# Reordering the tiles of the longest-lived SBUF pool in a one-layer trunk kernel: u and y ahead of con, rb and par

## The chip, the cores and the metric

The kernel runs on one core of one Trainium2 chip. The metric is the device time of one execution in microseconds; below 0.2% two versions can hardly be told apart here. Engines are named as in the profile: PE is TensorE's matmul, PEld its weight load, DVE is VectorE, ACT is ScalarE, POOL is GpSimd, SP is SyncE, which starts the DMAs.

## The reference, cut to what matters

One layer of a hybrid encoder trunk for 256 tokens of width 2048, all in float32:

```
u = rmsnorm(x, norm_mix_g)
z = u @ w_in                       # 2048 x 5140, four head groups
y = concat(short_gated_conv, multiscale_pool, gated_linear_attention, forgetting_attention)
x = x + y @ w_out                  # 2048 x 2048
u = rmsnorm(x, norm_ffn_g)
x = x + (silu(u @ w_gate) * (u @ w_up)) @ w_down   # 2048 x 5632, 5632 x 2048
```

Nearly all of the arithmetic is in the four large products. The head groups between them are small.

## The kernel before

**Number format.** Every factor of a large product is kept as two float32r parts: a high part, which is the value rounded, and a low part, which is the rest. A product is then three matmuls that add into the same PSUM bank (`three`, lines 135 to 139): weight-high by value-high (L137), weight-high by value-low (L138), weight-low by value-high (L139). Each loads its 128x128 stationary operand anew.

**Weights.** All large weights lie in DRAM as 380 chunks of 512 KB. `stage_through` (L101 to L114) brings a chunk into `raw`, ACT rounds it into `hi` (L113), and DVE subtracts to give `lo` (L114). `raw` has 3 buffers, `hi` and `lo` have 4 each; chunks are staged three ahead of their use. One chunk feeds 24 matmuls of 256 columns, or 12 of 512.

**Values.** `u` holds the normalized input as [128 partitions, 16 blocks of the model width, 2 parts, 256 tokens], `y` the mixer's output in the same shape, 32768 bytes per partition each. Both live in the pool `keep` for the whole kernel, with `xT` (the running x, transposed), `par` (54 columns of gains, biases and other parameters), `con` (960 columns of constants: identity, ones, masks), `rb` and `rcol` (the inverse norms).

**Stages in order.**

- The lead block (`block_lead`, L168) and one more block of 256 columns (`block_fm`): `u` is the moving operand.
- Five blocks of 512 columns (`block_tm`, L183 to L185): here `u` is the stationary operand and the weight parts `hi` and `lo` are the moving ones.
- Eight blocks of `block_fm` with `u` moving, then the output projection, eight blocks with `y` moving.
- Gate and up, 44 blocks with `u` (the first 4) or `y` (the other 40) moving; `y` has been overwritten by the normalized input.
- Down, 8 blocks over the 5632 hidden columns. The high parts of the hidden values overwrite `u` and then `y`; the low parts lie in eleven tiles `hl` of the pool `ffn`, which opens when the mixer's pools have closed. So of each three matmuls two have `u` or `y` as moving operand and the middle one has `hl`.

Small matmuls of the head groups (attention scores, transposes, gates) are placed between the large ones by a list of tasks, a step or two after each chunk. Two of them are named below: L635 multiplies `wsm`, a weight that lies in the room of `y` for a while, as stationary operand by 512 columns of `u`, sixteen times in a row; L526 multiplies a small `sel` by 256 columns of `fhl`, both float32r tiles of the pool `mx`.

**Where a tile lies.** In a pool with one buffer per tile, the tiles lie one behind another in the order in which they are first asked for, each one starting at the next multiple of 32 bytes within a partition. The pools lie one behind another too.

Of the kernel before, what the change touches and what calls it, by code (L numbers as in the profile page):

```python
# [9 lines left out]
F32 = mybir.dt.float32  # L10
# [7 lines left out]
P = 128  # L18
# [19 lines left out]
NPAR = 54  # L38

C_ID, C_ONE, C_CAUS, C_RST, C_CNT, NCON = 0, 128, 384, 640, 896, 960  # L40
# [19 lines left out]
def trunk_kernel(ctx: ExitStack, tc: tile.TileContext, a, out):  # L60
# [3 lines left out]
    keep = ctx.enter_context(tc.tile_pool(name="keep", bufs=1))  # L64
# [10 lines left out]


    xT = keep.tile([P, KT, T], F32, name="xT")
    par = keep.tile([P, NPAR], F32, name="par")
    con = keep.tile([P, NCON], F32, name="con")
    u = keep.tile([P, KT, 2, T], F32R, name="u")  # L80
    y = keep.tile([P, KT, 2, T], F32R, name="y")
    rb = keep.tile([P, T], F32, name="rb")
    rcol = keep.tile([P, 2], F32, name="rcol")

    mixer = ExitStack()
# [769 lines left out]
```

## Time and profile before

| | |
|---|---|
| median of 3 runs | 1118.85 us (1117.97 to 1119.15) |
| the profiled execution | 1118.63 us |
| its span, first to last instruction | 1116.8 us |
| PE busy | 1107.4 us, 99% |
| PEld busy | 1073.3 us, 96% |
| DVE busy | 634.6 us, 57% |
| ACT busy | 487.4 us, 44% |
| DMA | 204.09 MB, mean 183 GB/s |

The span leaves 1.8 us of the execution outside. Matmuls overlap in the records: one is listed with some 281 ns, while the next starts some 118 ns after it. So a matmul's cost on the path is the step from its start to the next one's start, and a busy PE says nothing on whether PE runs at its best.

### The profile page before, as it was taken

Reading aid. Unit: us, or ns where it says so; the run is one execution under the profiler, and the core shown is the slowest. Engines: PE = TensorE matmul, PEld = TensorE weight load, DVE = VectorE, ACT = ScalarE, POOL = GpSimd, SP = SyncE. Lnnn points to the kernel's source line nnn. Section 1 sums busy time; section 2 is a strip of 40 time slices with the busy share of each in tenths; the row PEclk is TensorE's granted clock in tenths of the full one; section 3 lists DMA queues with packets and bytes.
Section 4 is the critical chain, followed back from the end, with each engine's and each line's share of the span. In section 5 each row is a group of like instructions: output and inputs, shape, how many; then the busy total and the mean of one; then the engine's idle time right before and its main releaser. Section 6 shows DMA issues by size and latency. Waiting matters only on the chain.

```text
span 1116.8 us, 20632 instructions
## 1 busy us (share of the span) xinstructions
PE 1107.4 (99%) x8836; PEld 1073.3 (96%) x8836; DVE 634.6 (57%) x744; ACT 487.4 (44%) x577; POOL 7.0 (1%) x12
## 2 busy tenths in 40 slices
PE   9999999999999999999999999999999999999998
PEld 7777779999999999999999999999999999999998
DVE  7797785688565684445545445454445444444442
ACT  6645453444454554444434434343434433333331
POOL 0000000001000000000000000000000000000000
PEclk9999999999999999999999999999999999999999
DMA  8554445444555556555555555555555566666562
GB/s 302 175 177 153 157 148 184 162 160 151 189 189 184 175 182 195 185 184 183 187 189 189 186 183 181 188 189 189 184 182 186 186 198 198 198 196 193 193 197 82
DMA packets 58908, 204.09 MB, mean 183 GB/s; under 512 B 6576, under 2 KB 8768, under 8 KB 58816
## 3 DMA queue, kind: packets, MB, share of 16 engines
q1 hardware_dynamic: 58672, 202.74, 55.5%
q8 instruction: 69, 1.13, 0.4%
q14 instruction: 23, 0.19, 0.0%
q10 hardware_dynamic: 144, 0.03, 0.0%
HBM read 200.65 MB, written 2.10 MB: 182 GB/s over the span
## 4 chain that ended last, share of the span: by engine, by line
PE 95%; DVE 3%; DMA 1%; issue 1%; ACT 0%; ACTq 0%; DVEq 0%
PE acc L139 28%; PE acc L137 28%; PE acc L138 28%; PE acc L183 3%; PE acc L184 3%; PE acc L185 3%; DVE lo L114 1%; PE misc L383 1%; DMA xT<-in_xT 1%; DMA raw<-in_wall 1%; DMA par<-in_par 0%; ACT hi L113 0%; PE misc L544 0%; PE misc L606 0%; DVE fe L310 0%
## 5 line engine op out<-in xcount | busy, mean ns | idle before, releaser
L114 DVE TENSOR_TENSOR lo<-raw,hi 128x1024 fp32r<-128x1024 f32 (+1 forms) x380 | 462.2, 1218 | 430.8 <-ACT hi L113 429.9
L113 ACT CAST hi<-raw 128x1024 fp32r<-128x1024 f32 (+1 forms) x380 | 394.8, 1040 | 579.5 <-PE acc L138 502.7
L139 PE MATMUL acc<-y,lo 128*128 128x256 f32 x1728 | 485.8, 281 | 0.0
L137 PE MATMUL acc<-y,hi 128*128 128x256 f32 x1728 | 485.7, 281 | 0.0
L138 PE MATMUL acc<-y,hi 128*128 128x256 f32 x1536 | 431.7, 281 | 0.0
L139 PEld LDWEIGHTS acc<-y,lo 128*128 128x128 f32 x1728 | 325.5, 188 | 0.0
L137 PEld LDWEIGHTS acc<-y,hi 128*128 128x128 f32 x1728 | 325.5, 188 | 0.0
L138 PEld LDWEIGHTS acc<-y,hi 128*128 128x128 f32 x1536 | 289.4, 188 | 0.1
L137 PE MATMUL acc<-u,hi 128*128 128x256 f32 x928 | 263.0, 283 | 0.0
L139 PE MATMUL acc<-u,lo 128*128 128x256 f32 x928 | 261.6, 282 | 0.8 <-DVE lo L114 0.8
L138 PE MATMUL acc<-hl,hi 128*128 128x256 f32 x704 | 195.4, 278 | 0.0
L139 PEld LDWEIGHTS acc<-u,lo 128*128 128x128 f32 x928 | 174.5, 188 | 1.0 <-DVE lo L114 1.0
L137 PEld LDWEIGHTS acc<-u,hi 128*128 128x128 f32 x928 | 174.5, 188 | 0.6 <-ACT hi L113 0.2
L138 PEld LDWEIGHTS acc<-hl,hi 128*128 128x128 f32 x704 | 132.2, 188 | 0.0
L138 PE MATMUL acc<-u,hi 128*128 128x256 f32 x416 | 116.9, 281 | 0.0
L138 PEld LDWEIGHTS acc<-u,hi 128*128 128x128 f32 x416 | 78.4, 189 | 0.1
L183 PE MATMUL acc<-hi,u 128*128 128x512 f32 x160 | 65.3, 408 | 0.0
L184 PE MATMUL acc<-hi,u 128*128 128x512 f32 x160 | 63.9, 400 | 0.0
L185 PE MATMUL acc<-lo,u 128*128 128x512 f32 x160 | 63.8, 399 | 0.0
L183 PEld LDWEIGHTS acc<-hi,u 128*128 128x128 f32 x160 | 30.3, 190 | 8.1 <-issue 0.3
L185 PEld LDWEIGHTS acc<-lo,u 128*128 128x128 f32 x160 | 30.4, 190 | 7.4
L184 PEld LDWEIGHTS acc<-hi,u 128*128 128x128 f32 x160 | 30.4, 190 | 6.6
(198 smaller groups left out, 407.7 us busy)
## 6 DMA issues: line engine op xcount, KB each, us to landing
raw<-in_wall SPq DMA_DIRECT2D x372, 512.0 KB, 3.6
xT<-in_xT SPq DMA_DIRECT2D x8, 256.0 KB, 5.5
raw<-in_wall SPq DMA_DIRECT2D x8, 256.0 KB, 5.7
out_T<-g SPq DMA_DIRECT2D x7, 256.0 KB, 4.1
con<-in_con SPq DMA_DIRECT2D x1, 480.0 KB, 5.0
msk_raw<-in_msk SPq DMA_DIRECT2D x1, 448.0 KB, 5.8
poolw<-in_poolw SPq DMA_DIRECT2D x1, 256.0 KB, 5.8
out_T<-n SPq DMA_DIRECT2D x2, 128.0 KB, 1.7
```

Of the source, the lines that this page charges most:

```text
L113: S.copy(out=hi[:, c], in_=raw[:, c])
L114: V.tensor_tensor(out=lo[:, c], in0=raw[:, c], in1=hi[:, c].bitcast(F32), op=ALU.subtract)
L137: PE.matmul(o, lhsT=hi, rhs=x[0], start=first, stop=False, skip_group_check=True)
L138: PE.matmul(o, lhsT=hi, rhs=x[1], start=False, stop=False, skip_group_check=True)
L139: PE.matmul(o, lhsT=lo, rhs=x[0], start=False, stop=last, skip_group_check=True)
L183: PE.matmul(b[t], lhsT=u[:, k, 0, ts], rhs=hi[:, kk], start=k == 0, stop=False)
L184: PE.matmul(b[t], lhsT=u[:, k, 1, ts], rhs=hi[:, kk], start=False, stop=False)
L185: PE.matmul(b[t], lhsT=u[:, k, 0, ts], rhs=lo[:, kk], start=False, stop=k == KT - 1)
L383: PE.matmul(banks[h % 2][:, c * P:(c + 1) * P], lhsT=ke[b, h // 2, st * P:(st + 1) * P], rhs=qe[b, h // 2, tt * P:(tt + 1) * P], start=Tru ...
```

## The change

The two parts of the pool that are not a multiple of 64 bytes long, `par` (216 bytes, 224 with rounding) and with it `con`, no longer lie ahead of `u` and `y`:

```diff
     xT = keep.tile([P, KT, T], F32, name="xT")
-    par = keep.tile([P, NPAR], F32, name="par")
-    con = keep.tile([P, NCON], F32, name="con")
+
     u = keep.tile([P, KT, 2, T], F32R, name="u")
     y = keep.tile([P, KT, 2, T], F32R, name="y")
+    con = keep.tile([P, NCON], F32, name="con")
     rb = keep.tile([P, T], F32, name="rb")
+    par = keep.tile([P, NPAR], F32, name="par")
     rcol = keep.tile([P, 2], F32, name="rcol")
```

The starts of the tiles in a partition, in bytes, as the two built programs have them:

| tile | before | modulo 64 | after | modulo 64 |
|---|---|---|---|---|
| xT | 16512 | 0 | 16512 | 0 |
| par | 32896 | 0 | 103296 | 0 |
| con | 33120 | 32 | 98432 | 0 |
| u | 36960 | 32 | 32896 | 0 |
| y | 69728 | 32 | 65664 | 0 |
| rb | 102496 | 32 | 102272 | 0 |
| rcol | 103520 | 32 | 103520 | 32 |
| hi, lo (8 buffers) | 115840 to 144512 | 0 | the same | 0 |
| fhl (2), sel | 166080, 167104, 168128 | 0 | the same | 0 |
| hl (11 tiles) | 174400 to 215360 | 0 | the same | 0 |

The pool keeps its length, so every tile of every other pool stays where it was. The pieces of `u`, `y`, `hl`, `hi` and `lo` that a matmul reads begin at multiples of 512 bytes within their tiles, so a piece has its tile's place modulo 64. Engine by engine, the instructions of the two programs stand in the same order and are the same but for these addresses; line numbers behind the pool's tiles are higher by 1 after the change.

## Rows read from the trace of the kernel before

**Rows 1.** The page: span, busy us (share, instructions) by engine, and PE's granted clock.

```profile
span 1116.8 us, 20632 instructions
...
PE 1107.4 (99%) x8836; PEld 1073.3 (96%) x8836; DVE 634.6 (57%) x744; ACT 487.4 (44%) x577; POOL 7.0 (1%) x12
...
PEclk9999999999999999999999999999999999999999
```

**Rows 2.** The page: chain that ended last, share of the span by engine and by line.

```profile
PE 95%; DVE 3%; DMA 1%; issue 1%; ACT 0%; ACTq 0%; DVEq 0%
PE acc L139 28%; PE acc L137 28%; PE acc L138 28%; PE acc L183 3%; PE acc L184 3%; PE acc L185 3%; DVE lo L114 1%; PE misc L383 1%; DMA xT<-in_xT 1%; DMA raw<-in_wall 1%; DMA par<-in_par 0%; ACT hi L113 0%; PE misc L544 0%; PE misc L606 0%; DVE fe L310 0%
```

**Rows 3.** Groups of PE's instructions: line, shapes, count | busy us, mean ns | idle before.

```profile
L139 PE MATMUL acc<-y,lo 128*128 128x256 f32 x1728 | 485.8, 281 | 0.0
...
L139 PE MATMUL acc<-u,lo 128*128 128x256 f32 x928 | 261.6, 282 | 0.8 <-DVE lo L114 0.8
L138 PE MATMUL acc<-hl,hi 128*128 128x256 f32 x704 | 195.4, 278 | 0.0
...
L183 PE MATMUL acc<-hi,u 128*128 128x512 f32 x160 | 65.3, 408 | 0.0
```

**Rows 4.** Timeline of PE in gate and up, 24 steps apart: start us, us, instruction.

```profile
599.78 0.28 PE L137 MATMUL acc<-y,hi 128*128 128x256 f32 x1
...
602.62 0.28 PE L137 MATMUL acc<-y,hi 128*128 128x256 f32 x1
```

**Rows 5.** Windows, PE alone: stretch, length, busy us (instructions), clock, DMA share, GB/s.

```profile
500.00:800.00 300.00, 300.00 (x2538) 1.00 0.57 186
900.00:1100.00 200.00, 200.00 (x1700) 1.00 0.60 194
```

**Rows 6.** Timeline of PE in down.

```profile
899.95 0.28 PE L137 MATMUL acc<-u,hi 128*128 128x256 f32 x1
900.07 0.28 PE L138 MATMUL acc<-hl,hi 128*128 128x256 f32 x1
900.18 0.28 PE L139 MATMUL acc<-u,lo 128*128 128x256 f32 x1
900.30 0.28 PE L137 MATMUL acc<-u,hi 128*128 128x256 f32 x1
900.42 0.28 PE L138 MATMUL acc<-hl,hi 128*128 128x256 f32 x1
900.54 0.28 PE L139 MATMUL acc<-u,lo 128*128 128x256 f32 x1
900.66 0.28 PE L137 MATMUL acc<-u,hi 128*128 128x256 f32 x1
900.78 0.28 PE L138 MATMUL acc<-hl,hi 128*128 128x256 f32 x1
900.89 0.28 PE L139 MATMUL acc<-u,lo 128*128 128x256 f32 x1
```

**Rows 7.** Tile hl: count, duration ns min/median/max, first and last start us.

```profile
L138 PE MATMUL acc<-hl,hi x704: 277/278/282, 864.7 to 1113.1; 128*128 128x256 f32 x176
```

**Rows 8.** Timeline of PE in the blocks of 512 columns, 24 steps apart.

```profile
160.75 0.40 PE L183 MATMUL acc<-hi,u 128*128 128x512 f32 x1
...
166.35 0.40 PE L183 MATMUL acc<-hi,u 128*128 128x512 f32 x1
```

**Rows 9.** Timeline of PE around L635, sixteen in one row.

```profile
33.96 3.81 PE L635 MATMUL acc<-u,y 128*128 128x512 f32 x16
37.62 0.40 PE L183 MATMUL acc<-hi,u 128*128 128x512 f32 x1
```

**Rows 10.** Timeline of PE at L526 over windows of growing length: one, then all four.

```profile
208.32 0.38 PE L526 MATMUL misc<-fhl,sel 4*128 4x256 f32 x1
208.32 0.73 PE L526 MATMUL misc<-fhl,sel 4*128 4x256 f32 x4
```

**Rows 11.** Waits of PE: line, releaser: us in total, times, longest us.

```profile
PE misc L482 <- DVE ob L473: 1.9, 1, 1.9
PE misc L217 <- DVE sq L284: 1.4, 1, 1.4
PE misc L243 <- DVE idle L239: 1.2, 1, 1.2
PE acc L139 <- DVE lo L114: 0.8, 1, 0.8
```

**Rows 12.** Windows: stretch, length, PE, PEld, DVE, ACT, POOL busy us (instructions), clock, DMA.

```profile
62.00:137.00 75.00, 75.00 (x415) 58.91 (x414) 60.52 (x89) 35.38 (x41) 0.00 (x0) 1.00 0.50 167
520.00:840.00 320.00, 320.00 (x2707) 320.00 (x2706) 153.00 (x146) 131.25 (x146) 0.00 (x0) 1.00 0.57 185
```

## The prediction, as it stood before the changed kernel was run

> **What bounds the kernel now.** I read the page first, then the groups of PE's instructions, then PE's timeline at five places. PE is busy for 99% of the span at a granted clock that never leaves its upper level for a whole slice [rows 1], and the chain that ended last lies on PE for 95%, nearly all of it in the lines of the large products [rows 2]. PE's waits for other engines are four, 5.3 us in all [rows 11]. So the time is the number of matmuls times the step from one start to the next, and the only thing the change can move on the path is that step. The counts: L139 runs 1728 + 928 = 2656 times with 256 columns, and L137 and L138 as often, of which 704 of L138 have `hl` moving [rows 3]; that is 704 groups of three in down and 7968 - 2112 = 5856 matmuls outside it, all with `u` or `y` moving. L183 to L185 are 480 matmuls of 512 columns.
>
> The steps. In gate and up 24 steps take 2.84 us [rows 4], 118.3 ns each; the count over 300 us says the same, 300 us / 2536 = 118.3 (two or three of the 2538 began before the window) [rows 5]. In down the first and the last of 704 `hl` matmuls are 248.4 us apart [rows 7]: 353.3 ns per group of three, 117.8 each. In the 512-column blocks 24 steps take 5.60 us [rows 8]: 233.3 ns.
>
> [...]
>
> **What the trace says about place.** Down has an experiment built in: same weights, same stationary operands, same shape; only the middle matmul's moving operand lies at 0 modulo 64, where the weights lie too, and the other two lie at 32. The step that begins with an `hl` matmul is read as 0.11, 0.12, 0.11 us, the two others as 0.12 each time [rows 6]. Over all 704 from the first to the last [rows 7] the starts in the trace give 114.2 ns from `hl` to the next, 120.0 from L137 to `hl`, 119.3 from L139 to L137. The records agree in length: 278 ns against 281 and 282 [rows 3].
>
> A second place with 512 columns: L635 has both operands at 32 modulo 64 and takes (37.62 - 33.96) / 16 = 228.8 ns [rows 9]; L183 has its stationary operand at 32 and its moving one at 0 and takes 233.3 [rows 8]. So not the place of one operand alone but a like place of both goes with the short step, in both pairs. After the change both operands lie at 0 in every large product.
>
> A third place speaks against it: L526 has both operands at 0, and its second to fourth end 1.05 - 0.70 = 0.35 us apart from the first, 117 ns each [rows 10], as in the mixed case. [...]
>
> **The change part by part.** It removes and adds no instruction, moves none, and adds no wait. The terms are:
>
> - 5856 matmuls outside down: 118.3 becomes 114.2, the step that the matched operands of down have. 5856 x 4.1 ns = 24.0 us. [...]
> - 704 groups in down: 353.3 becomes 3 x 114.2 = 342.6. 704 x 10.7 = 7.5 us. [...]
> - 480 matmuls of 512 columns: 233.3 becomes 228.8, as L635 has it. 480 x 4.5 = 2.2 us. [...]
> - The lead block's 96 and the first 30 us wait for loads: nothing taken.
> - `con`, `par` and `rb` also move. They are read by small ACT and DVE work and by a few dozen small matmuls. DVE and ACT sit idle for 43% and 56% of the span [rows 1], which covers a few ns either way; I take nothing.
>
> Sum 33.7 us; 1118.6 of the profiled execution less 33.7 gives **1085 us** (that execution lies 0.2 us under the median, so nothing is added).
>
> What could hand some of it back: a chunk's 24 matmuls would take 2.74 us instead of 2.84. In gate and up DVE is busy for 153 of 320 us and ACT for 131, the DMA engines for 57% [rows 12], so the weights' supply has room several times over. In the gated attention DVE is busy for 60.5 of 75 us [rows 12], 81%, and PE's waits at L482 and L217 lie around there [rows 11]. That stretch would gain only some 2 to 3 us, so that is all that can be lost.
>
> [...] The built programs show that before and after every piece of `u` and `y` begins on a multiple of 32 bytes and covers 1024 bytes without a gap; [rows 6] has shorter steps for the operand that lies on 64. [...]
>
> **The rivals.**
>
> 1. *No change: 1118.6.* The short step of `hl` would come from something else that sets it apart: it lies in another tile than its neighbours, and higher in memory. For it: L526 with 117 ns in spite of matched operands [rows 10]. Against it: L635 reads `u` and `y`, low in memory, and also has short steps [rows 9]. That the change does not do what it says is ruled out by the addresses of the built program.
> 2. *A smaller gain: 1105.* A start may be recorded later or earlier with the place of the operand. Then only the sum of the three steps is real: 353.3 - 2 x 118.3 = 116.7 for the matched one. 5856 x 1.6 = 9.4, 704 x (353.3 - 350.1) = 2.3, and 0 to 2.2 for the 512 columns: 12 to 14 us. For it: the steps into `hl` are longer than 118.3, as if lent.
> [...]
> 4. *Slower: 1133.* The step depends on the operand that is about to start, and 114.2 is the price of a mismatched one behind a matched one, while 120, the step into `hl`, is the price of a matched moving operand [rows 6]. All at 120: 5856 x 1.7 = 10.0 and 704 x (360 - 353.3) = 4.7, together 14.7 us more. It decides as soon as every step ends at a matched operand, which is everywhere after the change. Against it: the three steps together are shorter than three without `hl`, 353.3 against 354.9.
>
> **How the numbers follow.** The forecast, 1074 to 1095, gets 0.53: two independent pairs of rows show the matched step, with 256 and 512 columns. The smaller gain, 1095 to 1111, gets 0.28. No change gets 0.11, the larger gain 0.04, slower 0.04. The range 1074 to 1111 takes in the first two, 0.81. Faster by over 0.2% is 0.53 + 0.28 + 0.04 = 0.85, within 0.2% (about what a measurement of this kernel can tell from no change) 0.11, slower 0.04.
>
> **What would show it.** In the timeline of gate and up, 24 steps in about 2.74 us instead of 2.84, all alike; the count of PE in 300 us of that stage about 2630 instead of 2538; in down the first and last `hl` matmul 241 us apart instead of 248.4; in the 512-column blocks 24 steps in 5.49 us instead of 5.60; instruction counts as before, DVE's and ACT's busy time too. A step of 116 to 117 in gate and up says the second rival, 118.3 the first, 120 the fourth. The prediction is wrong in its mechanism if `hl` keeps a step that differs from its neighbours', and wrong in its cover if PE's waits for DVE in the first 170 us grow by more than 3 us.

## The result, and the profile after the change

The changed kernel takes 1124.59 us (median of 6 runs, 1122.85 to 1128.24) against 1118.22 us (6 runs, 1117.11 to 1119.15): a ratio of 1.0067, 95% interval 1.0054 to 1.0080. It is slower by 0.7%, a small loss but clear of the spread, where 1085 us was forecast. Lines of the changed kernel are higher by 1: L138 to L140 are the three matmuls of a large product, L184 to L186 those of the 512-column blocks.

The page of the changed kernel, span, busy time by engine and the chain that ended last; they answer to [rows 1, 2]:

```profile
span 1122.3 us, 20632 instructions
...
PE 1112.7 (99%) x8836; PEld 1082.1 (96%) x8836; DVE 634.5 (57%) x744; ACT 487.0 (43%) x577; POOL 6.9 (1%) x12
...
PE 94%; DVE 2%; DMA 2%; ACT 1%; issue 0%; SPq 0%; ACTq 0%; DVEq 0%
```

The same instructions, DVE and ACT as busy as before, the bound still PE. So it is again the step from one matmul to the next. The windows of PE alone (stretch, length, busy us and instructions, clock, DMA share, GB/s), to be read beside [rows 5]:

```profile
500.00:800.00 300.00, 300.00 (x2503) 1.00 0.56 184
900.00:1100.00 200.00, 200.00 (x1701) 1.00 0.61 196
```

In gate and up there are 2503 matmuls in 300 us where there were 2538; in down as many as before. The timeline of PE gives the steps: in gate and up, 24 steps apart, as [rows 4]; then 18 steps apart in the 512-column blocks, as [rows 8]:

```profile
599.46 0.28 PE L139 MATMUL acc<-y,hi 128*128 128x256 f32 x1
...
602.34 0.28 PE L139 MATMUL acc<-y,hi 128*128 128x256 f32 x1
```

```profile
160.67 0.39 PE L184 MATMUL acc<-hi,u 128*128 128x512 f32 x1
...
164.75 0.39 PE L184 MATMUL acc<-hi,u 128*128 128x512 f32 x1
```

And the tile `hl` (count, ns min/median/max, first and last start), as [rows 7]; 703 steps of a group lie between its first and last start:

```profile
L139 PE MATMUL acc<-hl,hi x704: 279/280/286, 870.2 to 1118.6; 128*128 128x256 f32 x176
```

| step, ns | before | forecast | after |
|---|---|---|---|
| 256 columns, gate and up | 118.3 | 114.2 | 2.88 us / 24 = 120.0 |
| group of three in down | 353.3 | 342.6 | 248.4 us / 703 = 353.3 |
| 512 columns, L183 to L185 | 233.3 | 228.8 | 4.08 us / 18 = 226.7 |

From these steps: 5856 x 1.7 = 10.0 us lost, nothing in down, 480 x 6.6 = 3.2 us gained, together 6.8 us longer by this estimate. The two profiled spans differ by 5.5 us, the medians by 6.4.

### The profile page after: what moved, and what is told of

Same layout as the page of the kernel before. It is cut to its first block, busy times and chain, and to the rows that moved or that the text cites. A ratio compares the mean times of both kernels' runs of the same rounds, so it can differ in the third digit from the quotient of the medians.

```text
span 1122.3 us, 20632 instructions
## 1 busy us (share of the span) xinstructions
PE 1112.7 (99%) x8836; PEld 1082.1 (96%) x8836; DVE 634.5 (57%) x744; ACT 487.0 (43%) x577; POOL 6.9 (1%) x12
## 4 chain that ended last, share of the span: by engine, by line
PE 94%; DVE 2%; DMA 2%; ACT 1%; issue 0%; SPq 0%; ACTq 0%; DVEq 0%
PE acc L139 28%; PE acc L138 28%; PE acc L140 28%; PE acc L184 3%; PE acc L185 3%; PE acc L186 3%; DMA raw<-in_wall 1%; DVE lo L115 1%; PE misc L384 1%; DMA xT<-in_xT 1%; ACT hi L114 1%; PE misc L545 0%; PE misc L607 0%; DVE fe L311 0%; DVE lsw L301 0%
## 5 line engine op out<-in xcount | busy, mean ns | idle before, releaser
L114 ACT CAST hi<-raw 128x1024 fp32r<-128x1024 f32 (+1 forms) x380 | 394.6, 1039 | 584.7 <-PE acc L139 509.5
L138 PE MATMUL acc<-y,hi 128*128 128x256 f32 x1728 | 488.6, 283 | 0.0
L140 PE MATMUL acc<-y,lo 128*128 128x256 f32 x1728 | 488.5, 283 | 0.0
L140 PEld LDWEIGHTS acc<-y,lo 128*128 128x128 f32 x1728 | 331.1, 192 | 0.0
L138 PEld LDWEIGHTS acc<-y,hi 128*128 128x128 f32 x1728 | 331.1, 192 | 0.0
L139 PEld LDWEIGHTS acc<-y,hi 128*128 128x128 f32 x1536 | 294.9, 192 | 0.1
L138 PE MATMUL acc<-u,hi 128*128 128x256 f32 x928 | 263.0, 283 | 0.0
L140 PE MATMUL acc<-u,lo 128*128 128x256 f32 x928 | 261.4, 282 | 0.8 <-DVE lo L115 0.8
L139 PE MATMUL acc<-hl,hi 128*128 128x256 f32 x704 | 198.0, 281 | 0.0
L140 PEld LDWEIGHTS acc<-u,lo 128*128 128x128 f32 x928 | 176.3, 190 | 1.0 <-DVE lo L115 1.0
L138 PEld LDWEIGHTS acc<-u,hi 128*128 128x128 f32 x928 | 176.2, 190 | 0.4
L139 PE MATMUL acc<-u,hi 128*128 128x256 f32 x416 | 117.8, 283 | 0.0
L139 PEld LDWEIGHTS acc<-u,hi 128*128 128x128 f32 x416 | 79.8, 192 | 0.1
L184 PE MATMUL acc<-hi,u 128*128 128x512 f32 x160 | 63.9, 399 | 0.0
L186 PE MATMUL acc<-lo,u 128*128 128x512 f32 x160 | 62.5, 391 | 0.0
L185 PE MATMUL acc<-hi,u 128*128 128x512 f32 x160 | 62.5, 390 | 0.0
L184 PEld LDWEIGHTS acc<-hi,u 128*128 128x128 f32 x160 | 30.0, 188 | 7.1 <-issue 0.3
L186 PEld LDWEIGHTS acc<-lo,u 128*128 128x128 f32 x160 | 30.0, 188 | 6.4
L185 PEld LDWEIGHTS acc<-hi,u 128*128 128x128 f32 x160 | 30.1, 188 | 5.8
```

The source lines that it names most:

```text
L114: S.copy(out=hi[:, c], in_=raw[:, c])
L138: PE.matmul(o, lhsT=hi, rhs=x[0], start=first, stop=False, skip_group_check=True)
L139: PE.matmul(o, lhsT=hi, rhs=x[1], start=False, stop=False, skip_group_check=True)
L140: PE.matmul(o, lhsT=lo, rhs=x[0], start=False, stop=last, skip_group_check=True)
L184: PE.matmul(b[t], lhsT=u[:, k, 0, ts], rhs=hi[:, kk], start=k == 0, stop=False)
L185: PE.matmul(b[t], lhsT=u[:, k, 1, ts], rhs=hi[:, kk], start=False, stop=False)
```

## The experiments

**Words.** The *distance* is the address of a matmul's moving operand less that of its stationary one, modulo 256 bytes. From the table of addresses ahead of the prediction: `u` and `y` against `hi` and `lo` stood at 224 before and stand at 0 after the change; `hl` against them stands at 192 in both. In the 512-column blocks, where `hi` and `lo` move, it was 32 and is 0.

### u and y 64 bytes further

```diff
     xT = keep.tile([P, KT, T], F32, name="xT")
+    keep.tile([P, 16], F32, name="pad_ahead")
     ...
     rcol = keep.tile([P, 2], F32, name="rcol")
+    keep.tile([P, 112], F32, name="pad_behind")
```

> The changed kernel with 64 bytes of room ahead of u and 448 behind rcol, so u and y lie 64 bytes past the weights' place modulo 512 (hi and lo at 128, u and y at 192; before: 96, changed: 128). All are still at 0 modulo 64. Theory A, the distance between moving and stationary operand counts modulo 64: distance 0 as in the changed kernel, step in gate and up 120 ns, 1124 us. Theory B, the distance counts modulo 128 or more, and only a distance of 0 is slow: the step is the one that hl had in the kernel before, 114 ns (hl lies 192 past the weights modulo 512, so 64 modulo 128), about 1085 us. Theory C, the moving operand's own place modulo 64 counts: as A, 1124 us.

Measured: 1094.81, 1094.95 and 1095.66 us in three runs, 1112.82 and 1114.50 in two. All five lie below the kernel before; the three shorter ones give a ratio of 0.980 (0.977 to 0.983). So theories A and C fall: all operands still lie at 0 modulo 64, and the time is another one. B's 1085 is not met either: the profiled run, of 1112.82 us, shows 2549 matmuls in the 300 us, 117.8 ns each, where the changed kernel has 2503 and 120.0:

```profile
500.00:800.00 300.00, 300.00 (x2549) 1.00 0.57 187
```

That one program has two times was new, and the later runs follow it up.

### Everything at 32 modulo 64

```diff
     xT = keep.tile([P, KT, T], F32, name="xT")
+    keep.tile([P, 8], F32, name="pad_ahead")
```

> The changed kernel with 32 bytes of room ahead of u and nothing behind, so u, y, hi, lo and hl all lie at 32 modulo 64 and all distances are as in the changed kernel (0 between u or y and the weights). Theories A and B, only the distance counts: step 120 ns in gate and up, 1124 us. Theory C, the place modulo 64 counts: step 118.3 as in the kernel before, 1118 us.

Measured: 1125.35 us, in one run. Its window in gate and up:

```profile
500.00:800.00 300.00, 300.00 (x2503) 1.00 0.55 183
```

The count is the changed kernel's to the instruction, though now neither `u` and `y` nor the weights begin on a multiple of 64. The place of an operand by itself counts for nothing here; C falls a second time.

### A scan of distances, nothing else running

Each row is one line of the kernel, one pair of places; `X` holds the moving pieces, `W` the stationary ones, and the numbers are the offsets in bytes:

```
for k, m in KM: PE.matmul(o(m), lhsT=hi(k, m, 0), rhs=x(k, 0, 192), **one); PE.matmul(o(m), lhsT=hi(k, m, 0), rhs=x(k, 1, 192), **mid); PE.matmul(o(m), lhsT=lo(k, m, 0), rhs=x(k, 0, 192), **end)
```

> Computes no layer at all: 31 rows of 96 matmuls of 256 columns in the kernel's pattern of three (stationary hi, hi, lo of 128 columns; moving first part, second part, first part), one row for each pair of places, and 6 rows of 48 matmuls of 512 columns; nothing else runs beside them. Base addresses of both tiles are equal modulo 512, so the offset in bytes is the distance. Theory A: steps of 120 at distances 0, 64, 128, 192 and on, 118.3 at 32, 96, 160. Theory B: 120 at 0 and 512 only (or at multiples of 128 or 256, which tells the modulus), 114 at 64 and 192. Theory C: 120 for each moving operand at a multiple of 64 and 118.3 for one at 32, wherever the weights are. If all rows are alike, the step is not set by the two operands' places but by something else running in the kernel. 512 columns: 226.7 at distance 0 and 233.3 at 32 by all three.

The timeline of PE; the difference of two starts by 96 (by 48 for 512 columns) is the step. L110 is at distance 32, L111 at 64 and on in steps of 32 to L117 at 256, then L118 at 320 and on in steps of 64 to L121 at 512; L127 has both offsets at 32, L128 is at distance 224 and L129 at 192 with the weights shifted in place of the moving operand, and L131 at 160 in the same way; L130 has both offsets at 64; L134 and L135 mix the distances of a group of three, 0, 192, 0 and 64, 192, 64; L138 is at 0 once more; L140 and L141 have 512 columns.

```profile
31.55 11.47 PE L110 MATMUL b<-X,W 128*128 128x256 f32 x96
42.87 11.47 PE L111 MATMUL b<-X,W 128*128 128x256 f32 x96
54.18 11.67 PE L112 MATMUL b<-X,W 128*128 128x256 f32 x96
65.69 11.55 PE L113 MATMUL b<-X,W 128*128 128x256 f32 x96
77.08 11.43 PE L114 MATMUL b<-X,W 128*128 128x256 f32 x96
88.34 11.07 PE L115 MATMUL b<-X,W 128*128 128x256 f32 x96
99.25 11.52 PE L116 MATMUL b<-X,W 128*128 128x256 f32 x96
110.61 11.68 PE L117 MATMUL b<-X,W 128*128 128x256 f32 x96
122.12 11.47 PE L118 MATMUL b<-X,W 128*128 128x256 f32 x96
133.43 11.55 PE L119 MATMUL b<-X,W 128*128 128x256 f32 x96
144.82 11.05 PE L120 MATMUL b<-X,W 128*128 128x256 f32 x96
155.71 11.66 PE L121 MATMUL b<-X,W 128*128 128x256 f32 x96
167.21 11.56 PE L122 MATMUL b<-X,W 128*128 128x256 f32 x96
...
224.65 11.68 PE L127 MATMUL b<-X,W 128*128 128x256 f32 x96
236.17 11.52 PE L128 MATMUL b<-X,W 128*128 128x256 f32 x96
247.53 11.05 PE L129 MATMUL b<-X,W 128*128 128x256 f32 x96
258.42 11.66 PE L130 MATMUL b<-X,W 128*128 128x256 f32 x96
269.91 11.55 PE L131 MATMUL b<-X,W 128*128 128x256 f32 x96
281.30 11.55 PE L132 MATMUL b<-X,W 128*128 128x256 f32 x96
...
304.10 11.49 PE L134 MATMUL b<-X,W 128*128 128x256 f32 x96
315.43 11.47 PE L135 MATMUL b<-X,W 128*128 128x256 f32 x96
326.73 11.47 PE L136 MATMUL b<-X,W 128*128 128x256 f32 x96
...
349.44 11.68 PE L138 MATMUL b<-X,W 128*128 128x256 f32 x96
360.95 11.47 PE L139 MATMUL b<-X,W 128*128 128x256 f32 x96
372.27 11.09 PE L140 MATMUL b<-W,X 128*128 128x512 f32 x48
383.19 11.35 PE L141 MATMUL b<-W,X 128*128 128x512 f32 x48
394.38 11.36 PE L142 MATMUL b<-W,X 128*128 128x512 f32 x48
```

| distance, bytes | 0 | 32 | 64 | 96 | 128 | 160 | 192 | 224 | 256 |
|---|---|---|---|---|---|---|---|---|---|
| step, 256 columns, ns | 119.9 (L138) | 117.9 | 117.8 | 119.9 | 118.6 | 117.3 | 113.6 | 118.3 | 119.9 |

The rows at 320, 384, 448 and 512 repeat those at 64, 128, 192 and 0: 117.8, 118.6, 113.4, 119.8. Shifting the weights gives the same as shifting the moving operand the other way: L128 118.3 at 224, L129 113.4 at 192. Only at 160 the two ways differ, 118.6 (L131) against 117.3 (L114). Both shifted alike is distance 0: 120.0 (L127) and 119.7 (L130). So the distance modulo 256 decides, B, and A and C have no row for them. The scan returns the kernel's steps with the other engines idle and the DMA engines too (a share of 0.00 in these rows): 118.3 at 224 as before, 120 at 0 as after. At 192 it has 113.4, near the 114.2 that the prediction read behind `hl`, though that reading does not hold, as the account below shows. What runs beside is not the cause. With 512 columns the order is another one: 227.5 at distance 0 (L140), 233.1 at 224 (L141). Distance 32, which these blocks had in the kernel before, is not among the rows of 512 columns.

Mixed groups have a step of their own. L134 has the distances that down has after the change, and its (315.43 - 304.10) / 96 = 118.0 ns, 117.8 behind the first 24, agree with the 353.3 ns per group of three in down. L135 gives (326.73 - 315.43) / 96 = 117.7.

### u and y at the distance of hl

```diff
     xT = keep.tile([P, KT, T], F32, name="xT")
+    keep.tile([P, 48], F32, name="pad_ahead")
     ...
     rcol = keep.tile([P, 2], F32, name="rcol")
+    keep.tile([P, 16], F32, name="pad_behind")
```

> The changed kernel with 192 bytes of room ahead of u and 64 behind rcol: u and y lie at 64 modulo 256 and hi and lo at 128, so the moving operand lies 192 past the stationary one modulo 256, as hl does, the distance with the shortest row of the scan (113.3 ns). Theory B (the distance modulo 256): step 113.3 in gate and up, 340 ns per group of three in down, and 229 ns in the 512-column blocks, whose distance is 64: 5856 x 5.0 = 29.3, 704 x 13.3 = 9.4, 480 x 4.3 = 2.1, together 40.8 us under the kernel before: 1078 us. Theory C (a multiple of 64 for the moving operand is bad in itself): 120 ns, 1124 us.

Measured: 1082.64 us (4 runs, 1078.25 to 1084.53), ratio 0.967, 95% interval 0.965 to 0.970: faster than both kernels. The forecast of 1078 is met by the shortest run. The windows of the profiled run, whose time was 1084.53 us, and its `hl`, (1079.1 - 840.0) / 703 = 340.1 ns per group:

```profile
300.00:360.00 60.00, 60.00 (x512) 1.00 0.56 185
500.00:800.00 300.00, 300.00 (x2649) 1.00 0.61 195
900.00:1070.00 170.00, 170.00 (x1503) 1.00 0.62 199
```

```profile
L140 PE MATMUL acc<-hl,hi x704: 276/276/276, 840.0 to 1079.1; 128*128 128x256 f32 x176
```

Gate and up and down run at 113.3 from some 380 us on, but between some 240 and 380 us the step is 117.8 (512 in 60 us) wherever no small matmuls stand between. That accounts for the 6 us over 1078, by an estimate: about 130 us / 117.8 = 1100 matmuls, times 4.5 ns, is 5 us.

### The kernel before, and 32 bytes behind its pool

```diff
     rcol = keep.tile([P, 2], F32, name="rcol")
+    keep.tile([P, 8], F32, name="pad_behind")
```

> The kernel BEFORE, its order of tiles untouched, with 32 bytes of room behind rcol. u and y keep their old addresses, at 32 modulo 64; hi, lo and everything behind move up by 32 bytes, so that the distance becomes 192 modulo 256. Theory B: as uy192, step 113.3 and 1078 us, though no operand of a large product lies on a multiple of 64. Theory that 64-byte starts matter: 118.3 or more, 1118 us or more.

Measured: 1078.30 and 1079.12 us in two runs, 1109.45 and 1109.63 in two. `u` and `y` have not moved, they still lie at 32 modulo 64, and 32 bytes that nobody uses take 9 to 40 us off the kernel before. That settles the direction: the starts at multiples of 64 are not what matters. The profiled run is the first of the four; those of 1109 us were not profiled:

```profile
300.00:360.00 60.00, 60.00 (x532) 1.00 0.62 194
500.00:800.00 300.00, 300.00 (x2649) 1.00 0.61 194
```

### One part undone: par ahead of u again

```diff
     xT = keep.tile([P, KT, T], F32, name="xT")
+    par = keep.tile([P, NPAR], F32, name="par")
     ...
-    par = keep.tile([P, NPAR], F32, name="par")
```

> The changed kernel with one part of the change undone: par lies ahead of u again, con stays behind y. par takes 224 bytes; con is 15 times 256 bytes long. By theory B moving con alone changes no distance modulo 256 (u and y at 224 past the weights, as before): step 118.3 in gate and up, 1118 us, no difference from the kernel before. If con's place mattered by itself, the time would be nearer the changed kernel's 1124.

Measured: 1117.04 us (10 runs, 1115.40 to 1118.92), ratio 0.9988 (0.9979 to 0.9997); gate and up as before:

```profile
500.00:800.00 300.00, 300.00 (x2538) 1.00 0.58 186
```

So the whole loss comes from moving the 224 bytes of `par`. `con` moved at a price within 0.2% of nothing; it is 3840 bytes long, 15 times 256, and so does not belong to the parts whose length is no multiple of 64, among which the section on the change counts it.

### Two lasting rhythms

Theory R says that at some distances the stream has two lasting steps and that a break in it decides which one follows; theory S, that each distance has one step and the spread of the times has another cause.

> The kernel with u and y 64 past the weights a second time, for its profile: three of five runs took 1095 us and two 1113, and the profile showed one of the latter, with 117.8 ns in gate and up. If the step has two lasting rhythms at this distance, a run near 1095 shows some 115 in gate and up and in down; if the difference lies in one stage or in a wait, gate and up stays at 117.8.

> The kernel before with 32 bytes behind rcol once more, for a profile of its longer time: two of four runs took 1078 us and two 1109. Theory R: a run near 1109 shows 117.8 in gate and up and 353 per group of three in down with the same waits; a run near 1078 shows 113.3 and 340 again. Theory S: the extra 31 us lie in waits or in one stage.

> u and y 64 past the weights, a third look for a profile of the shorter time. Both profiles so far are near 1113 us with 117.8 ns in gate and up, but each shows some 115.6 ns for 20 us around 200 us. If that is the second rhythm of this distance and it can last to the end, a run near 1095 shows about 115.6 in gate and up and in down: (117.8 - 115.6) x 7968 = 17.5 us less. If the shorter time comes from one stage alone, gate and up stays at 117.8.

The second run for a profile of 64 took 1113.87 us and has 117.8 again in gate and up; only from 22 to 30 us it has 113.3, where the first has 117.8. The second one of the kernel before with 32 bytes took 1083.77 us, neither of its two times, and its profile has both steps one behind the other. The third one of 64 took 1095.18 us. Its windows, behind those of old32_again:

```profile
300.00:360.00 60.00, 60.00 (x512) 1.00 0.58 186
500.00:800.00 300.00, 300.00 (x2650) 1.00 0.60 195
```

```profile
300.00:360.00 60.00, 60.00 (x512) 1.00 0.57 189
500.00:800.00 300.00, 300.00 (x2650) 1.00 0.61 195
900.00:1070.00 170.00, 170.00 (x1446) 1.00 0.59 195
```

At 64 the stream goes at 117.8 to some 380 us, at 113.3 (300 us / 2648) to some 840 us, and at 117.8 through down. The expected 115.6 throughout is wrong in size and place, though the sum fits as well: 450 us / 113.3 = some 3970 matmuls times 4.5 ns is 18 us. In the window from 500 to 800 us this run has 2650 matmuls where the first profile of the same program has 2549, both at a granted clock of 1.00, so the clock does not make the two times. The changes of step at some 240 and 380 us lie where small matmuls break the stream. The one at some 840 us has no break: it comes with the first `hl` matmul of down, where the distances become 64, 192, 64, and that mix has 117.7 in the scan (L135). So down says nothing on the two steps of distance 64. The 1109 us of old32 have no profile; that they are 117.8 nearly throughout fits the time (31 us / 4.5 ns is 6900 of 7968 matmuls) but was not shown.

Whether a break decides was tested by itself, on rows of 72 with one to three float32 matmuls of 128 columns ahead of each:

> Computes no layer: rows of 72 matmuls as in the scan, each row behind one to three float32 matmuls of 128 columns that break the stream, as the small matmuls do in the kernel. Eight distances four times each. Theory R (at some distances the stream has two lasting rhythms and a break decides which): 120 at distance 0 and 118.3 at 224 each time, but both 113.3 and 117.8 at 192 and both 117.8 and a lower one at 64. Theory S (one step per distance, the kernel's spread has another cause): the four rows of a distance agree. A row with hi at 0 and lo at 64, first moving part at 192 and second at 0: if the distance to the weights loaded beside the matmul (those of the next one) counts, all three are at 192: 113.3 or 117.8; if the distance to its own weights counts, they are 192, 0 and 128: about 118 to 119, no 113.3. [...]

The timeline of PE at its four rows of distance 192 (start, length):

```profile
82.16 8.42 PE L138 MATMUL b<-X,W 128*128 128x256 f32 x72
...
153.68 8.73 PE L154 MATMUL b<-X,W 128*128 128x256 f32 x72
...
225.72 8.42 PE L170 MATMUL b<-X,W 128*128 128x256 f32 x72
...
297.02 8.42 PE L186 MATMUL b<-X,W 128*128 128x256 f32 x72
```

Same places, same instructions, and one of four rows 0.31 us longer: read from the starts behind the first 24, the three run at 113.3 and the fourth at 117.8. At distance 0 all rows run at 120.0, at 224 all at 118.4. That is theory R for 192; at 64 all four rows gave 117.8, so its second rhythm is seen in the kernel alone.

Two more results of this kernel, both read from the starts behind the first 24 of a row. In its rows at distance 0, 320 columns take 146.7 ns, 384 take 173.3, 448 take 202.7 and 512 take 226.7. From 320 to 512 that is 80.0 ns for 192 columns, 0.417 ns each; at this rate, an estimate from these two rows, what is left of each step over its columns is 13.3 ns, and 16.0 with 448 columns. A share of the columns would have taken the 120.0 ns of 256 columns to 240.0 with 512. So at these lengths it is an amount per matmul, not a share of the columns. With 320 columns the distance changes nothing (146.6 to 146.7 at 0, 64, 192 and 224). The rows with three matmuls at 192 from the next one's weights, but at 192, 0 and 128 from their own, ran at 118.4 to 118.6 and never at 113.3. In the trace of the kernel before, the load for L138 in down and the matmul L137 ahead of it both start at 899.95 us, so the next weights are loaded beside a matmul. But the distance to these weights does not alone decide; which of the neighbouring loads and streams meet was not found out.

## Why the prediction was wrong

**The bound** was right: PE, and only the step between matmuls. So was the cover of DVE, ACT and DMA: PE's waits for other engines went from 5.8 to 6.2 us (the prediction's four of 5.3 us leave out a fifth of 0.5). So was the price of zero for the places of `con`, `par` and `rb` as such: in uy192 they lie in the new order behind `y`, in old32 in the order of the kernel before, and the shortest runs of the two are 1078.25 and 1078.30 us.

**The step that failed** is the one from the rows of down to a rule. [rows 6, 7] do show a short step behind an operand that lies elsewhere. I read its place modulo 64, because the change is written in multiples of 64, and took a like place of both for what made it short. The table of addresses had the modulus open: `hl` is 192 from the weights modulo 256, and the change puts `u` and `y` at 0, a distance that no 256-column row of a large product had. The scan gives 113.4 to 113.6 at 192 and 119.7 to 120.0 at 0. Nor was 114.2 the price of `hl`'s place: after the change `hl` lies at 192 as before, and the starts in the trace give 117.7 ns from `hl` to the next, 118.1 into `hl` and 117.5 between the other two, in a group of 353.3 ns as before. One step in a mixed group is not the price of one operand. So the forecast of 114.2 for a stream all alike had no ground in these rows; that a stream all at 192 does take 113.3 was not to be had from them.

**The second pair of rows** was carried over wrongly. L635 has distance 0 and 512 columns, and the last nine of its steps settle at 226.7 ns. Half of that, 113.3 of 256 columns, was my estimate of how far the gain could go; that the step goes with the columns was not shown. By the rows of 320 to 512 columns it is 0.417 ns a column plus 13.3 ns, which makes 120.0 of 256 by this estimate, the very step that came. Two lengths at the same distance would have told a share from an amount; before had only the one. The one 256-column row at distance 0 in the trace, L526 with 117 ns [rows 10], was the nearest case to the change in its places. It spoke against the gain, and I gave it little weight because it was short; but it did not announce the loss either, for 117 is not 120.

**By terms.** 24.0 us gain outside down: 10.0 us loss by the measured steps, the sign wrong for the reason above. 7.5 us gain in down: measured 0. There the distances went from 224, 192, 224 to 0, 192, 0 and the group of three kept its 353.3 ns: the mix has its own step, as L134 of the scan shows, and the steps of single operands can't be added up. 2.2 us gain in the 512-column blocks: 3.2 by the measured steps. That this term came is luck: the reason given for it, a like place modulo 64, is the one that failed, and distance 0 happens to be the shortest of those tried with 512 columns.

**The rivals.** No change was nearest in time; it was right that something other than a like place modulo 64 sets `hl` apart, but that is the distance and not, as it says, the tile or the height in memory. The doubt of the second, whether more than the sum of the three steps in down is to be trusted, is borne out by the new split of the 353.3 ns; its gain did not come. The fourth, 1133 us, named the step that gate and up took, 120 ns, and its sign was right; its mechanism, the operand about to start, is not what the scan shows, and in down its 360 ns did not come. The larger gain, with its 0.04, came in no run: the shortest time of all variants is 1078.25 us and the shortest step of 256 columns 113.3 ns, so no run comes to the 1074 us at which the range begins.

**The cause.** The scan shows steps of 113.4 to 120.0 ns among distances that are all multiples of 32 bytes. In it no other engine works (a DMA share of 0.00 in its rows), and the step still hangs on where the two operands lie to one another. Whether the two reads hinder one another was not shown, only that the distance sets the step; the cause behind it stays open.

## What to carry to other kernels

Where float32r matmuls of 256 columns followed one another without a gap, each with a new stationary operand, place counted in these runs as the distance between the moving and the stationary operand, with steps of 113.3 to 120.0 ns, not as the start of either: take both addresses from the built program and compare them modulo 256 before believing in an alignment. A short stand-alone scan, one line per distance, answers in 450 us of device time what a trace with two or three distances can't. Read an extra cost at two operand lengths before scaling it, and don't take one step of a mixed group for the price of one operand: only the sum of the group is sure. A row that disagrees at the very case of the change, however short, is a reason to measure that case by itself first.

## What the runs showed of the hardware

- With float32r, 256 columns and a new 128x128 stationary operand each time, the step is 113.3 to 120.0 ns by the distance modulo 256, as far as it is a multiple of 32: up to 6% of a kernel that is nothing but such matmuls, by an estimate from these steps. The kernel before had 118.3 in gate and up; with 32 unused bytes it had 113.3 there in its best run.
- With 512 columns distance 0 is the shortest of those tried, 226.7 against 228.9 at 64 and 233.3 at 192 and 224; with 256 columns it is, with 96, the longest of the multiples of 32. With 320 columns none of the four distances tried differs.
- At distances of 64 and 192 one and the same stream has two lasting steps, 113.3 and 117.8 ns, and in these traces it goes from one to the other where small matmuls break it. One program takes 1095 or 1113 us by it; that the 1078 and 1109 us of another come from it too was not shown. At 32 and 160 the rows differ by a ns among themselves (117.8 and 116.7, 117.3 and 118.6), so more distances may have this. At 0 and 224 nothing of it was seen: all four rows run at 120.0 there, and all four at 118.4.
- A distance of 4 bytes gives the longest step of the scan behind its first row, 123.2 ns (L124 of the scan).
